# Fetching routing weights from DRAM instead of spreading them with TensorE, for two early row blocks of a soft mixture of experts

## The chip, the core and the metric

The kernel runs on one core of a Trainium2 chip. The metric is the device time of one execution in microseconds, from the first to the last instruction. A core has TensorE (PE in the profile, with its weight loads as PEld), VectorE (DVE), ScalarE (ACT), GpSimd (POOL) and SyncE (SP). SP issues most of the DMAs, on a hardware queue (q1 in the profile); GpSimd issues those that change the type of the data, on a software queue (q0). Both queues are served by the same 16 DMA engines.

## What is computed

Each token has a softmax over eight experts, and its output is the sum of all eight experts' products, weighted by that softmax.

```python
probs = softmax(router_logits)              # 16 x 512 tokens, 8 experts
output = zeros(16, 512, 2048)
for e in range(8):
    output += probs[:, :, e:e+1] * (x @ expert_weights[e])   # 512 -> 2048
```

The kernel uses that a routing weight may be multiplied into x first. With z_e = p_e x, the whole is one matrix product of 8192 rows (tokens), an inner length of 8 x 512 = 4096, and 2048 columns.

## The kernel before

**The work as a whole.** The big product is cut in two by two by two (256-row blocks with an even and an odd number, experts 0 to 3 and 4 to 7, the left and the right 1024 columns), and a seven-product scheme (Strassen-Winograd) takes the place of the eight block products. Several of those products are cut in the same way again inside: `sub_product` (L370) takes two row blocks, forms four products z of x and routing weights with `mul` (L344), four sums and differences of them, and from these runs seven inner products p1 to p7 of two times eight matmuls (once for each 128 rows). The inner operands are named in the table `z` there: p1 takes a11, p2 a12, p5 s1, p6 s2, p3 s4, p7 the difference a11 - a21, p4 a22; they run in this order. Matmuls are fp16, 128 x 128 by 128 x 512, and add up in fp32 in the eight PSUM banks. Intermediate results go to DRAM (`kept`).

**The order of the work.** Almost all DVE and ACT instructions of the start are pinned to the order in which the program writes them (`dve`, L114). Within an engine instructions run in order. DMAs are placed on their queue by a scheduler, and a DMA that must wait holds up everything behind it on the queue of the engine that issues it. Buffers of the pool `h` are handed out by hand: `share` (L78) gives each use those that were taken longest ago.

**How the kernel starts.** Eight tiles of 128 rows of x lie in `xs0`: four of row blocks 0 and 2, four of row blocks 4 and 6. In row terms the second four are 1024 to 1279 and 1536 to 1791.

- The first four tiles get their routing weights by TensorE: x is multiplied with a diagonal matrix of the weights (`diag`, L250; `early_z0`, L269), which transposes and weights it in one step. Their product runs plainly in the loop over `n` from L442, in two halves of 512 columns.
- The second four tiles must become what `sub_product` wants: x transposed (`xT`), and the routing weights of each token spread over all 128 partitions (`pT`). `early_xp1` (L284) does both with TensorE during the second half of that loop: four matmuls with the identity give a transposed tile, and one matmul of a matrix of ones with four diagonals side by side gives the spread weights. DVE evicts the first from PSUM, ACT the second. The weights for it come from a small softmax of these rows alone (`early_p(1)`), from logits that have been loaded for it in the right layout.
- All later blocks take another way. `softmax_of_all` (L308) computes the routing weights of all rows and writes them with four stores to `p_dram` (L297), in a layout from which `load_p` (L339) fetches a block's weights with one DMA that repeats them on every partition.

After the loop, `sub_product(1, 0, P1, ...)` (L480) runs over the row blocks 4 and 6 first, with `xp1` handed to it, and then over later ones, which it loads itself. Between its first operations on DVE lie three sums of weights (`inner_sums`, L173) that p5, p6 and p7 need.

Of the kernel before, what the change touches and what calls it, by code (L numbers as in the profile page):

```python
# [32 lines left out]
def kernel(  # L33
# [7 lines left out]
    nc = tc.nc  # L41
    P = 128
    f16 = mybir.dt.float16
    f32 = mybir.dt.float32
# [4 lines left out]
    E, _, EH = expert_weights.shape  # L49
    T = B * S  # L50
    C = H // P
    HE = E // 2
# [3 lines left out]
    HQ = 256  # L56
# [10 lines left out]
    xpool = ctx.enter_context(tc.tile_pool(name="xpool", bufs=8))  # L67
    hpool = ctx.enter_context(tc.tile_pool(name="hpool", bufs=1))
    cpool = ctx.enter_context(tc.tile_pool(name="cpool", bufs=1))
# [8 lines left out]
    def share(**sizes):  # L78

        order = sorted(used, key=used.get)  # L80
        for use, n in sizes.items():
            places[use], order = [order[:n], 0], order[n:]

    def h_tile(shape, dtype, use="any"):
        mine, i = places[use]
        places[use][1] = (i + 1) % len(mine)
        used[mine[i]] = next(turn)
        return hpool.tile(shape, dtype, name="h", tag=f"h{mine[i]}")
# [22 lines left out]
    def note(i):  # L111
        last[i.ins.engine] = i.ins

    def dve(i):  # L114
        note(i)
        if pinned[0]:
            tc.keep_in_program_order(i)
# [3 lines left out]
    def tt(o, a, b, op):  # L121
        dve(nc.vector.tensor_tensor(out=o, in0=a, in1=b, op=op))  # L122
# [9 lines left out]
    def sp(o, i):  # L132
        note(nc.sync.dma_start(out=o, in_=i))  # L133
# [4 lines left out]
    def bank():  # L138
        return psum.tile([P, NB], f32, name="ps", tag="ps")

    def mm(ps, z, w, start, stop):
        nc.tensor.matmul(ps, z, w, start=start, stop=stop, skip_group_check=True)  # L142
# [5 lines left out]
    def new_w():  # L148
        return wpool.tile([P, K8, NB], f16, name="w", tag="w")
# [23 lines left out]
    def inner_sums(b, t3=None):  # L173

        t3 = t3 or b[0, 1]
        w = {1: b[0, 0], 2: b[1, 0], 3: b[1, 1], 7: t3}

        def step(p, x, y):
            if p not in w:
                w[p] = new_w()  # L180
            tt(w[p], x, y, SUB)
        return w, [lambda: step(5, b[0, 1], b[0, 0]), lambda: step(6, b[1, 1], w[5]),
                   lambda: step(4, w[6], b[1, 0]), lambda: step(7, b[1, 1], b[0, 1])]
# [12 lines left out]
    def softmax(lg, J, pf=None):  # L196
        mx = h_tile([P, J], f32)
        dve(nc.vector.tensor_reduce(out=mx, in_=lg, axis=AX, op=mybir.AluOpType.max))
        tt(lg, lg, mx.unsqueeze(2).to_broadcast([P, J, E]), SUB)
        nc.scalar.activation(out=lg, in_=lg, func=mybir.ActivationFunctionType.Exp)  # L200
        sm = h_tile([P, J], f32)
        dve(nc.vector.tensor_reduce(out=sm, in_=lg, axis=AX, op=ADD))
        dve(nc.vector.reciprocal(out=sm, in_=sm))
        if pf is None:
            pf = h_tile([P, E, J], f32)
        n = pf.shape[1]
        tt(pf, lg.rearrange("p j e -> p e j")[:, 0:n], sm.unsqueeze(1).to_broadcast([P, n, J]), MUL)
        return pf

    lg_f = router_logits.flatten_outer_dims()  # L210
    P2, P1, PQ = 0, HE, 2 * HE
# [6 lines left out]
    def cast_x(j):  # L218
        pool(xs0[:, ds(j, 2), :], x_f[ds(j * HQ, HQ), :].rearrange(ROWS[j // 4], p=P))

    def load_lg0(t):
        rows = lg_f.rearrange("(q h) e -> q h e", h=2 * HQ)[ds(2 * t, 2), 0:HQ]
        tile_ = lg0[t].rearrange("p (q j) e -> p q j e", j=2)
        if t == 0:
            sp(tile_, rows.rearrange("q (p j) e -> p q j e", p=P))
        else:
            for q in range(2):
                sp(tile_[:, q], rows[q].rearrange("(j p) e -> p j e", p=P))
    lg0 = [cpool.tile([P, 4, E], f32, name=f"lg0_{t}") for t in range(2)]
    load_lg0(0)  # L230
    cast_x(0)
    cast_x(2)
    ident = cpool.tile([P, P], f16, name="ident")
# [10 lines left out]
    for e in range(2):  # L244
        cast_w(11, BLOCKS[3], e, b11[BLOCKS[3]])

    def early_p(t):
        return softmax(lg0[t], 4, cpool.tile([P, HE, 4], f16, name=f"ph0_{t}"))

    def diag(p):  # L250

        d = h_tile([P, 4, P], f16)
        tt(d, ident.unsqueeze(1).to_broadcast([P, 4, P]), p.to_broadcast([P, 4, P]), MUL)
        return d

    def evacuate(o, ps, i):
        if i % 2:
            act(nc.scalar.copy(o, ps))
        else:
            dve(nc.vector.tensor_copy(o, ps))  # L260


    z0 = [zpool.tile([P, HE, C, P], f16, name="z", tag="z") for j in range(4)]
    ph0 = [early_p(0)]

    def diag_e(e):
        return diag(ph0[0][:, e].unsqueeze(2))

    def early_z0(e, d):  # L269
        for j in range(4):  # L270
            ps = bank()
            for c in range(C):
                mm(ps[:, ds(c * P, P)], xs0[:, j, ds(c * P, P)], d[:, j], c == 0, c == C - 1)
            evacuate(z0[j][:, e], ps.rearrange("p (c t) -> p c t", c=C), j)


    ones = cpool.tile([P, P], f16, name="ones")
    nc.vector.memset(ones, 1.0)
    xp1 = [[xpool.tile([P, C, HQ], f16, name=name, tag="x") for name in ("xT", "pT")] for t in range(2)]

    def diag_j(j):
        return diag(ph0[1][:, :, ds(j % 4, 1)])

    def early_xp1(j, d):  # L284
        t, rows = j // 2 - 2, ds(j % 2 * P, P)
        ps = bank()
        for c in range(C):
            mm(ps[:, ds(c * P, P)], xs0[:, j, ds(c * P, P)], ident, c == 0, c == C - 1)
        evacuate(xp1[t][0][:, :, rows], ps.rearrange("p (c t) -> p c t", c=C), 0)
        ps = bank()  # L290
        mm(ps, ones, d.rearrange("p e t -> p (e t)"), True, True)
        evacuate(xp1[t][1][:, :, rows], ps.rearrange("p (e t) -> p e t", e=HE), 1)


    R = 4
# [4 lines left out]

    def load_logits():
        dve(nc.vector.memset(lg_all[:, 0, 0:1], 0.0))
        dve(nc.vector.memset(lg0[1][:, 0, 0:1], 0.0))
        load_lg0(1)
        for r in range(R):
            sp(lg_all[ds(r * NHQ, NHQ)], lg_v[r])

    def softmax_of_all():  # L308
        pf = softmax(lg_all, J)
        ph = h_tile([P, 3 * HE, J], f16)  # L310
        nc.scalar.copy(ph[:, 0:HE], pf[:, HE:E])
        nc.scalar.copy(ph[:, HE:2 * HE], pf[:, 0:HE])
        tt(ph[:, 2 * HE:], pf[:, 0:HE], pf[:, HE:E], ADD)
        for r in range(R):
            sp(p_dram[:, :, ds(r * J, J)], ph[ds(r * NHQ, NHQ)])
# [3 lines left out]
    x_new = []  # L319
# [19 lines left out]
    def load_p(h, first):  # L339
        pT = xpool.tile([P, HE, HQ], f16, name="pT", tag="x")  # L340
        sp(pT, p_dram[h, ds(first, HE), :].partition_broadcast(P))
        return pT
# [10 lines left out]
    def half(use="any"):  # L353
        return h_tile([P, NB], f32, use)
# [82 lines left out]
    ds_ = [diag_e(0), diag_e(1)]  # L437
# [4 lines left out]
    for n in range(2):  # L442
        ps = [bank() for _ in range(4)]
        for e in range(HE):
            if n == 0 and e < 2:
                early_z0(e + 2, ds_[e + 2])
                if e == 0:
                    ds_.append(diag_e(3))
            for c in range(C):
                for j in range(4):  # L450
                    mm(ps[j], z0[j][:, e, c], b11[e // 2, n][:, e % 2 * C + c, :],
                       e + c == 0, e == HE - 1 and c == C - 1)
            if n == 1:
                for j in ((4, 5), (6, 7), (), ())[e]:
                    early_xp1(j, ds_[j - 4])
                if e == 1:
                    sums[0]()
        for j in range(4):
            o = half()
            act(nc.scalar.copy(o, ps[j]))  # L460
            sp(kept[1][j // 2][n].rearrange("(p j) m -> j p m", j=2)[j % 2], o)
        if n == 0:
            ph0.append(early_p(1))
            softmax_of_all()
            ds_ = [diag_j(j) for j in range(4, 8)]
            w, sums = inner_sums(b11, new_w())

    def weights_of_t1():
# [6 lines left out]
        yield  # L475
        ready[5] = yield from inner_weights(b)
    pinned[0] = False
    x_new.extend((4 + 2 * t, xp1[t][0]) for t in range(2))
    share(xs=3, r=4, o=8)
    sub_product(1, 0, P1, w, weights_of_t1(), 1,  # L480
                xp1, (sums[1], sums[3], sums[2]))
# [115 lines left out]
    rows = Rows(0)  # L597
# [9 lines left out]
    for q in range(NI):  # L607
# [14 lines left out]
        for j, tn in enumerate(QUARTERS):  # L622
            if j > 1:
                rows.load_kept(j)
            x = bank()
# [34 lines left out]
        for j, tn in enumerate(QUARTERS):  # L660
            x, m5 = xs[j], rows.m5[tn]
# [17 lines left out]
        if q == 0:  # L679
# [15 lines left out]
            rows = following  # L695
            continue

        def prod(p, b):
            if b not in banks:
                banks[b] = bank()  # L700
            for k in range(K8):
                mm(banks[b], z3[p][:, k, :], inner3[p][:, k, :],
                   p in (1, 5) and k == 0, k == K8 - 1)
            return banks[b]
# [6 lines left out]
        x = prod(1, "x")  # L711
# [15 lines left out]
        if q < NI - 1:  # L727
            d = prod(4, "d")
# [3 lines left out]
        rows = following  # L732
# [35 lines left out]
```

## Time and profile before

| what | value |
|---|---|
| time, median of 3 runs | 1434.25 us (1433.23 to 1434.26) |
| profiled span | 1434.2 us |
| PE busy | 1424.9 us, 99% |
| DVE busy | 1032.0 us, 72% |
| ACT busy | 271.0 us, 19% |
| matmuls of z and weights, 128 x 512 and like it | 6560, 379 ns each from start to end |
| granted TensorE clock | 0.999 of full speed |
| DMA moved | 318.92 MB, mean 222 GB/s |

Busy shares are means over the whole span, and successive matmuls overlap in them. So the table tells which engine sets the pace, and not what happens in a stretch of a few microseconds. For that the timeline is read: each of its rows gives the start, the length, the engine, the line, the operation with output and inputs, the number of instructions merged, and in brackets how long the engine was idle before and what ended the wait. `L122` is the helper of all DVE operations on two tensors, `L142` that of all matmuls, `L133` and `L136` those of the DMAs of SP and GpSimd; which operation is meant is seen from the tiles. In the first 50 us the DMA engines are nearly full up to about 36 us with the first weights and x.

### The profile page before, as it was taken

How to read it: one execution, taken by the hardware profiler on the slowest of the kernel's cores; microseconds unless marked ns; L12 is line 12 of the kernel's file. 1: busy time of each engine (PE TensorE's matmuls, PEld its weight loads, DVE VectorE, ACT ScalarE, POOL GpSimd, SP SyncE). 2: the span in 40 equal slices, each digit the busy share in tenths (PEclk: the TensorE clock that was granted, in tenths of full speed). 3: DMA queues.
4: the chain of work that ended last, by engine and by line, in shares of the span. 5: the costliest groups of instructions: out<-in, count | busy, mean ns of one | idle time of the engine just before them, and what ended most of it. 6: DMA issues, size and time to landing. Idle time of an engine off the chain costs nothing.

```text
span 1434.2 us, 18172 instructions
## 1 busy us (share of the span) xinstructions
PE 1424.9 (99%) x6654; PEld 647.9 (45%) x6654; DVE 1032.0 (72%) x1173; ACT 271.0 (19%) x472; POOL 219.6 (15%) x344
## 2 busy tenths in 40 slices
PE   9999999999999999999999999999999999999998
PEld 4444444444444444444444444444444444444444
DVE  6967585656686867766767687777777877877773
ACT  3211111111111111111111211111111111111111
POOL 3111000110001000001000222222222222222220
PEclk9999999999999999999999999999999999999999
DMA  9899967899649994467766967777777767778764
GB/s 196 185 249 266 274 160 191 183 258 259 208 148 301 352 338 147 132 191 222 213 248 206 298 188 238 237 237 233 229 220 226 210 212 214 231 234 242 220 199 103
DMA packets 192041, 318.92 MB, mean 222 GB/s; under 512 B 51664, under 2 KB 80592, under 8 KB 187344
## 3 DMA queue, kind: packets, MB, share of 16 engines
q1 hardware_dynamic: 135328, 202.92, 44.2%
q0 software_dynamic: 56624, 114.84, 34.1%
q8 instruction: 52, 0.85, 0.2%
q14 instruction: 37, 0.30, 0.1%
HBM read 180.13 MB, written 159.58 MB: 237 GB/s over the span
## 4 chain that ended last, share of the span: by engine, by line
PE 93%; issue 3%; DMA 2%; POOL 1%; DVE 0%; ACT 0%; POOLq 0%; SPq 0%; DVEq 0%; ACTq 0%
PE ps L142 93%; POOL out_dram L595 1%; DMA h<-kept 1%; DMA out_dram<-h 1%; DMA w<-in_expert_weights_dram 1%; POOL w L136 0%; DVE z L122 0%; DVE h L122 0%; ACT ps L626 0%; SPq L133 0%; POOLq L595 0%; POOL ident L235 0%; DVEq L122 0%; POOLq L136 0%; POOLq L235 0%
## 5 line engine op out<-in xcount | busy, mean ns | idle before, releaser
L142 PE MATMUL ps<-w,z 128*128 128x512 f16 x6560 | 1415.2, 379 | 3.5 <-ACT ps L626 1.9
L142 PEld LDWEIGHTS <-z 128*128 128x128 f16 x6560 | 641.6, 98 | 776.0 <-issue 2.2
L122 DVE TENSOR_TENSOR h<-ps,h 128x512 f32<-128x512 f32 x389 | 267.7, 689 | 312.9 <-PE ps L142 89.2
L122 DVE TENSOR_TENSOR z<-xT,pT 128x2048 f16<-128x2048 f16 x252 | 304.2, 1218 | 32.5 <-PE ps L142 30.5
L122 DVE TENSOR_TENSOR z<-z 128x2048 f16<-128x2048 f16 x280 | 303.6, 1108 | 7.3
L404 ACT COPY h<-ps 128x512 f32<-128x512 f32 x248 | 145.3, 586 | 602.1 <-PE ps L142 594.9
L595 POOL DMA_DIRECT2D out_dram<-h x244 | 153.7, 663 | 535.4 <-DVE h L122 328.8
L122 DVE TENSOR_TENSOR w<-w 128x4096 f16<-128x4096 f16 x36 | 82.3, 2286 | 0.8 <-DMA w<-wd 0.7
L664 ACT COPY h<-ps 128x512 f32<-128x512 f32 x64 | 37.5, 585 | 177.0 <-PE ps L142 172.4
L136 POOL DMA_DIRECT2D h<-in_x_dram x30 | 21.3, 709 | 263.3 <-DMA xT<-h 226.2
L122 DVE TENSOR_TENSOR h<-h 128x512 f32<-128x512 f32 (+1 forms) x67 | 46.0, 687 | 20.8 <-DMA h<-kept 20.3
L122 DVE TENSOR_TENSOR h<-h,ps 128x512 f32<-128x512 f32 (+1 forms) x78 | 52.7, 675 | 11.0 <-PE ps L142 10.9
L136 POOL DMA_DIRECT2D w<-in_expert_weights_dram x41 | 30.8, 765 | 187.3 <-DVE w L161 131.0
L645 ACT ACTIVATE ps<-h 128x512 f32<-128x512 f32 x35 | 21.0, 602 | 166.9 <-DVE h L122 166.9
L626 ACT COPY ps<-h 128x512 f32<-128x512 f32 x64 | 35.6, 593 | 36.3 <-DMA h<-kept 30.7
L136 POOL DMA_DIRECT2D w<-wd x12 | 6.5, 543 | 189.1 <-DVE w L161 116.1
L724 ACT COPY h<-ps 128x512 f32<-128x512 f32 x15 | 8.8, 585 | 120.7 <-PE ps L142 120.7
L713 ACT COPY h<-ps 128x512 f32<-128x512 f32 x15 | 8.8, 586 | 16.5 <-PE ps L142 16.5
L260 DVE CAST z<-ps 128x512 f16<-128x512 f32 x8 | 5.2, 686 | 4.3 <-PE ps L142 4.3
L136 POOL DMA_DIRECT2D w<-wdt x8 | 4.4, 560 | 21.9 <-DVE w L161 21.9
L260 DVE CAST xT<-ps 128x512 f16<-128x512 f32 x4 | 2.6, 687 | 5.4 <-PE ps L142 5.4
L142 PEld LDWEIGHTS <-w 128*128 128x128 f16 x80 | 5.0, 98 | 2.6 <-DMA w<-in_x_dram 0.9
(37 smaller groups left out, 44.3 us busy)
## 6 DMA issues: line engine op xcount, KB each, us to landing
out_dram<-h POOLq DMA_DIRECT2D x244, 256.0 KB, 4.9
kept<-h SPq DMA_DIRECT2D x192, 256.0 KB, 4.1
h<-kept SPq DMA_DIRECT2D x192, 256.0 KB, 4.6
pT<-p_dram SPq DMA_DIRECT2D x124, 256.0 KB, 5.1
w<-in_expert_weights_dram POOLq DMA_DIRECT2D x39, 512.0 KB, 12.8
out_dram<-h SPq DMA_DIRECT2D x75, 256.0 KB, 3.4
xT<-x SPq DMA_DIRECT2D x62, 256.0 KB, 2.8
w<-wd POOLq DMA_DIRECT2D x12, 1024.0 KB, 10.7
```

The source lines that it names most:

```text
L122: dve(nc.vector.tensor_tensor(out=o, in0=a, in1=b, op=op))
L136: note(nc.gpsimd.dma_start(out=o, in_=i))
L142: nc.tensor.matmul(ps, z, w, start=start, stop=stop, skip_group_check=True)
L260: dve(nc.vector.tensor_copy(o, ps))
L404: nc.scalar.copy(t, ps)
L595: queue.dma_start(out=out_rows(self.q, odd, tn[0], cols, tn[1]), in_=o, **how)
L626: act(nc.scalar.copy(x, rows.m1[tn]))
L645: act(nc.scalar.mul(banks[b], v, scale))
L664: act(nc.scalar.copy(c21, x))
L713: act(nc.scalar.copy(r1, x))
L724: act(nc.scalar.copy(r3, x))
```

## The change

The routing weights of the row blocks 4 and 6 are now fetched from `p_dram` by `load_p`, as for all later blocks. TensorE only transposes their x. The small softmax, its logits' loads, the matrix of ones and the four diagonals of these rows are gone. The eviction of the four transposed tiles, once all on DVE, alternates between DVE and ACT. It is meant to relieve PE of four matmuls, DVE of the diagonals and the softmax, and ACT of two evictions.

```diff
-    def load_lg0(t):
-        rows = lg_f.rearrange("(q h) e -> q h e", h=2 * HQ)[ds(2 * t, 2), 0:HQ]
...
-    lg0 = [cpool.tile([P, 4, E], f32, name=f"lg0_{t}") for t in range(2)]
-    load_lg0(0)
+    lg0 = cpool.tile([P, 4, E], f32, name="lg0")
+    sp(lg0.rearrange("p (q j) e -> p q j e", j=2),
+       lg_f.rearrange("(q h) e -> q h e", h=2 * HQ)[0:2, 0:HQ].rearrange("q (p j) e -> p q j e", p=P))
...
-    ones = cpool.tile([P, P], f16, name="ones")
-    nc.vector.memset(ones, 1.0)
-    xp1 = [[xpool.tile([P, C, HQ], f16, name=name, tag="x") for name in ("xT", "pT")] for t in range(2)]
-
-    def diag_j(j):
-        return diag(ph0[1][:, :, ds(j % 4, 1)])
-
-    def early_xp1(j, d):
+    x1 = [xpool.tile([P, C, HQ], f16, name="xT", tag="x") for t in range(2)]
+
+    def early_x1(j):
         t, rows = j // 2 - 2, ds(j % 2 * P, P)
         ps = bank()
         for c in range(C):
             mm(ps[:, ds(c * P, P)], xs0[:, j, ds(c * P, P)], ident, c == 0, c == C - 1)
-        evacuate(xp1[t][0][:, :, rows], ps.rearrange("p (c t) -> p c t", c=C), 0)
-        ps = bank()
-        mm(ps, ones, d.rearrange("p e t -> p (e t)"), True, True)
-        evacuate(xp1[t][1][:, :, rows], ps.rearrange("p (e t) -> p e t", e=HE), 1)
+        evacuate(x1[t][:, :, rows], ps.rearrange("p (c t) -> p c t", c=C), j)
...
     def load_logits():
         dve(nc.vector.memset(lg_all[:, 0, 0:1], 0.0))
-        dve(nc.vector.memset(lg0[1][:, 0, 0:1], 0.0))
-        load_lg0(1)
...
                 for j in ((4, 5), (6, 7), (), ())[e]:
-                    early_xp1(j, ds_[j - 4])
+                    early_x1(j)
...
         if n == 0:
-            ph0.append(early_p(1))
             softmax_of_all()
-            ds_ = [diag_j(j) for j in range(4, 8)]
+            xp1 = [(x1[t], load_p(4 + 2 * t, P1)) for t in range(2)]
             w, sums = inner_sums(b11, new_w())
...
-    x_new.extend((4 + 2 * t, xp1[t][0]) for t in range(2))
+    x_new.extend((4 + 2 * t, x1[t]) for t in range(2))
```

More of the change, by code (lines that the diff above doesn't have):

```diff
@@ L219, in cast_x @@
         pool(xs0[:, ds(j, 2), :], x_f[ds(j * HQ, HQ), :].rearrange(ROWS[j // 4], p=P))
-    def load_lg0(t):
-        rows = lg_f.rearrange("(q h) e -> q h e", h=2 * HQ)[ds(2 * t, 2), 0:HQ]
[L223 to L228, printed above, removed]
-    lg0 = [cpool.tile([P, 4, E], f32, name=f"lg0_{t}") for t in range(2)]
-    load_lg0(0)
+    lg0 = cpool.tile([P, 4, E], f32, name="lg0")
+    sp(lg0.rearrange("p (q j) e -> p q j e", j=2),
+       lg_f.rearrange("(q h) e -> q h e", h=2 * HQ)[0:2, 0:HQ].rearrange("q (p j) e -> p q j e", p=P))
     cast_x(0)
@@ L245 @@
         cast_w(11, BLOCKS[3], e, b11[BLOCKS[3]])
-    def early_p(t):
-        return softmax(lg0[t], 4, cpool.tile([P, HE, 4], f16, name=f"ph0_{t}"))
     def diag(p):
@@ L263 @@
     z0 = [zpool.tile([P, HE, C, P], f16, name="z", tag="z") for j in range(4)]
-    ph0 = [early_p(0)]
+    ph0 = softmax(lg0, 4, cpool.tile([P, HE, 4], f16, name="ph0"))
     def diag_e(e):
-        return diag(ph0[0][:, e].unsqueeze(2))
+        return diag(ph0[:, e].unsqueeze(2))
     def early_z0(e, d):
```

## The prediction

> **What bounds the kernel now.** I read the page's busy shares first: PE 99% of 1434.2 us, DVE 72%, ACT 19%. So TensorE (PE) sets the end, and a change counts only by the matmuls it takes away and the waits it gives PE. Then the chain of waits over the first 100 us, because the edit touches only that stretch (columns: start, length, what):
>
> ```profile
> 10.80 35.64 PE ps L142 x188
> 46.44 0.78 issue
> 47.21 1.23 DVE z L122
> 48.44 0.05 issue
> 48.49 51.54 PE ps L142 x238
> ```
>
> PE runs without a break from 10.80, but at 48.49 it has waited for VectorE (DVE) to write a z tile. The PE timeline gives the size of that hole:
>
> ```profile
> 34.18 13.98 PE L142 MATMUL ps<-w,z 128*128 128x512 f16 x64
> 48.49 17.87 PE L142 MATMUL ps<-w,z 128*128 128x512 f16 x82 [0.33 <-DVE z L122]
> ```
>
> One matmul shows 0.379 us from start to end (its row on the page), so 64 of them start (13.98 - 0.379) / 63 = 0.2159 us apart; the 65th could have started at 34.18 + 64 x 0.2159 = 48.00. The hole is 0.49 us. The first 32 of these 64 are the end of the first product; from 41.09 follow the seven sub-products of the first two row blocks, eight matmuls (1.73 us) each, in the order p1, p2, p5, p6, p3, p7, p4. Matmul 65 is p3, and its operand is s4. The DVE timeline shows s4 as the last of a chain:
>
> ```profile
> 29.39 1.29 DVE L260 CAST xT<-ps 128x512 f16<-128x512 f32 x2 [4.83 <-PE ps L142]
> 30.79 2.36 DVE L122 TENSOR_TENSOR z<-xT,pT 128x2048 f16<-128x2048 f16 x2
> 33.73 1.29 DVE L260 CAST xT<-ps 128x512 f16<-128x512 f32 x2 [0.58 <-PE ps L142]
> 34.93 2.28 DVE L122 TENSOR_TENSOR w<-w 128x4096 f16<-128x4096 f16 x1
> 37.13 2.35 DVE L122 TENSOR_TENSOR z<-xT,pT 128x2048 f16<-128x2048 f16 x2
> 39.40 2.28 DVE L122 TENSOR_TENSOR w<-w 128x4096 f16<-128x4096 f16 x1
> 41.60 1.22 DVE L122 TENSOR_TENSOR z<-z 128x2048 f16<-128x2048 f16 x1
> 42.74 2.29 DVE L122 TENSOR_TENSOR w<-w 128x4096 f16<-128x4096 f16 x1
> 44.94 3.49 DVE L122 TENSOR_TENSOR z<-z 128x2048 f16<-128x2048 f16 x3
> ```
>
> From 33.73 to 48.43 DVE never rests, so here it is the bound, and everything hangs on when its first product with pT (30.79) may start. In the kernel before, pT came from PE and ScalarE (ACT) and was there in time. Last, the queue of SyncE (SP), with the times from issue to landing below it (median):
>
> ```profile
> 22.47 2.67 SPq L133 DMA_DIRECT2D p_dram<-h  x4
> 25.68 3.06 SPq L133 DMA_DIRECT2D kept<-h  x4
> ...
> p_dram<-h SPq DMA_DIRECT2D x4, 48.0 KB, 8.8
> ...
> kept<-h SPq DMA_DIRECT2D x4, 256.0 KB, 10.9
> ```
>
> These stores are slow because the 16 DMA engines are full with the weights and x of the other queue until about 34 (section 2 of the page: DMA 9 there). One by one, the p_dram stores took 6.7, 7.4, 8.8 and 10.1 us: the last, issued at 24.52, landed at 34.6. The last kept store, issued at 28.2, landed at 39.1. They landed in the order of issue.
>
> **What the Trainium skill says.** "DMA: Bandwidth & Descriptors", section "Queues, rings and completion order": each DMA engine serves the queue rows in turn, packet by packet, and takes the descriptors of one ring in order. The trace agrees: while the software queue was busy, p_dram's 1536 small packets crept through at some 190 per us, and the kept stores landed only behind them. The same page, "Two DMAs through the same engine are not ordered": a load of what an earlier DMA wrote must wait for that DMA's semaphore before it is issued. So load_p has to sit on SP until p_dram has landed. "TensorE: Matmul & The Clock Gate", section "Back-to-back issue gap", gives 2.5 ns above N / 2.4 for a warm matmul, 215.8 ns for 512 columns; measured 215.9. Its section "What's actually happening" says that an idle window of about 3.4 us halves the clock until about 3.4 us of work; the trace shows a cold start (10 warm-up matmuls in 4.43 us), but no idle time that long afterwards.
>
> **The change, part by part.**
>
> Taken from PE: four matmuls of ones with a diagonal, 4 x 0.2159 = 0.86 us. Taken from DVE: four diagonals (2.49 us at 22.07) and the small softmax (five operations from 15.89 to 17.20), plus memsets. The diagonals are worth nothing themselves, as DVE then waits until 29.39 for PE. The small softmax stood ahead of the large one; without it the large one can start when the last eviction ends at 15.98 instead of at 17.20. The logits (landed by 16.0, and without the many small pieces of the other load no later) don't hold it. So p_dram is written 1.2 us earlier: issued from 21.25, last landing 34.6 - 1.2 = 33.4.
>
> Moved: of the eight evictions four stay, two on DVE and two on ACT. DVE had four in the chain above; one of the two at 33.73 goes, 0.6 us of the chain after the first product.
>
> Added: two loads of pT, 256 KB each. In the changed kernel's instruction order they stand on SP's queue behind the four kept stores and wait for all four p_dram stores. SP is through with kept at 28.74, then stands until 33.4. Behind the loads stand the transposes of the next blocks' x, first needed much later (their product ran at 51.75). The loads go at 33.4 and about 33.9 into the ring behind 1 MB of kept, whose last store landed at 39.1. Two corrections of that: p_dram is 1.2 us earlier, so kept is too. And x's third load, which GpSimd (POOL) issued at 39.63 after waiting 17.97 us for a kept store to free its buffer, now has a buffer that waits for no store. So it goes out near 23, as soon as an earlier load on its lane has landed, and its 256 KB, about 1.3 us at the 205 GB/s that this stretch moved, take turns with kept. The two cancel: kept lands near 39.2. pT then needs one more transfer's time. The four kept stores landed from 36.7 to 39.1, 0.8 us apart, so pT lands at about 40.0 and the second at 40.8. **T = 40.0** is when DVE may start. Bounds: 33.4 plus the 3.1 us of the fastest pT load in the trace, 36.5; and 42 if the three queues' work adds up without overlap.
>
> DVE's sequence from there, with the steps as they were: both products take until T + 2.27 before the next operation starts, one eviction 0.6, then the stretch from 34.93 to 48.43 unchanged, 13.5. So s4 is ready at T + 16.4 and p3 starts then. It started at 48.49, so the loss is T + 16.4 - 48.49 = T - 32.1; at T = 40.0 that is **7.9 us**. The second pT is needed only at T + 5.1, when it is there. PE meets the wait in pieces: p1 waits for a11 until 41.2 (without the ones matmuls it could start at 40.2), p5 for s1 until T + 10.8 = 50.8 (p2 ends about 44.7: a hole of 6.1), p6 for s2 until 54.1 and p3 for s4 until 56.4. The 0.86 us that PE saves lie inside these holes and bring nothing. p4 needs its weights at T + 18.6 and starts at T + 19.9, so nothing more is lost. A hole of 6.1 us may halve the clock: p5 would then take 3.4 instead of 1.7 us, which fits ahead of s2; if it stayed cold through p6, some 1.2 us would be lost in addition. I take 0 for it and keep 1.2 for the range.
>
> Does the loss stay? After this PE runs without a hole to 842.9, and its chain there goes back to PE's own results; a delay at 48 shifts everything. DVE is late by as much, but the next blocks' operands had slack: the last one was ready at 63.0 for a p3 due at about 72.6. Sum: 1434.25 + 7.9 = 1442.2.
>
> **Rivals.** (B) pT passes the kept stores or they are quicker: T = 36.5, loss 4.4, 1438.7. For it: round-robin service and 400 GB/s once the weights are in. Against: one ring, landed in order. (C) pT is there when DVE wants it, T about 30.3: then the hole of 0.49 closes and 0.86 us of matmuls are gone, 1434.25 - 1.4 = 1432.9. For it: p_dram is issued at 21.25, nine microseconds ahead. Against: its own landing at 34.6. (D) The loss arises but a later wait takes it up, such as the 1.88 us at 842.9, which would have to shrink fully and more: about 1436.0. Against: that wait hangs on PE's own pace. (E) T = 42 and a cold clock: 9.9 + 1.2 = 11.1, 1445.4.
>
> **How the numbers follow.** Forecast 0.66, B 0.17, C 0.04, D 0.05, E 0.08. The range 1438.2 to 1444.6 takes in B and most between the forecast and E; it leaves out C, D and the end of E, with some spread around B. Only C and D lie within 0.2% (2.9 us): same 0.08; nothing found brings more than 1.4 us: faster 0.02; slower 0.90.
>
> **What would show it.** In the changed profile: the first product z<-xT,pT near 40 instead of 30.79, with DVE idle before it and pT from p_dram as releaser; PE idle some 9.3 us (7.9 + 0.49 + 0.86) in three or four pieces between 40 and 57; last p_dram landing near 33.4; SP's pT issues just after it; a third x load near 23. I am wrong if the first product starts near 30, if SP issues pT before 30, or if the later profile makes up for the delay.

## The result, and the profile after

| | median | runs | ratio to before |
|---|---|---|---|
| before | 1433.59 us | 6, 1433.05 to 1434.26 | |
| changed | 1445.22 us | 6, 1443.84 to 1446.53 | 1.0079, 95% interval 1.0066 to 1.0092 |

The change costs 11.6 us (9.5 to 13.2 by the interval). The forecast was 7.9, with a range up to 1444.6: the direction and the path (VectorE waiting for pT) were right, and the size was too small. The profiled spans are 1434.2 and 1443.3 us, only 9.1 apart. Where the other 2.5 us are is part of what follows.

The timeline of DVE in the changed kernel (start, length, engine, line, operation, count, idle time before and what ended it):

```profile
28.67 0.69 DVE L250 CAST xT<-ps 128x512 f16<-128x512 f32 x1 [7.71 <-PE ps L142]
41.20 2.36 DVE L122 TENSOR_TENSOR z<-xT,pT 128x2048 f16<-128x2048 f16 x2 [11.84 <-ACT h L440]
43.48 0.68 DVE L250 CAST xT<-ps 128x512 f16<-128x512 f32 x1
44.08 2.28 DVE L122 TENSOR_TENSOR w<-w 128x4096 f16<-128x4096 f16 x1
...
54.09 3.49 DVE L122 TENSOR_TENSOR z<-z 128x2048 f16<-128x2048 f16 x3
```

The eviction is over at 29.36, and DVE then stands for 11.84 us until its first product with pT: T = 41.20. The releaser that is named, an ACT copy, is a trap. Copies at line 440 write stage buffers, which the product doesn't read; the wait is for several semaphores at once and is put down to the event that came last. SP's queue shows what it was:

```profile
21.27 2.67 SPq L133 DMA_DIRECT2D p_dram<-h  x4
24.95 2.70 SPq L133 DMA_DIRECT2D kept<-h  x4
34.22 0.81 SPq L133 DMA_DIRECT2D pT<-p_dram  x2
```

And the DMA view has the time from issue to landing of the two loads (last column, the median):

```profile
pT<-p_dram SPq DMA_DIRECT2D x2, 256.0 KB, 7.0
```

The first load was issued at 34.22, when the last p_dram store had landed, and took 6.9 us: 41.1. In e_kept_act and the other variants with a load below, the same wait is put down to pT's load itself. PE:

```profile
42.49 5.01 PE L142 MATMUL ps<-w,z 128*128 128x512 f16 x16 [2.83 <-DVE z L122]
52.03 5.32 PE L142 MATMUL ps<-w,z 128*128 128x512 f16 x16 [4.53 <-DVE z L122]
57.64 2.55 PE L142 MATMUL ps<-w,z 128*128 128x512 f16 x11 [0.29 <-DVE z L122]
```

p1 and p2 wait for the first products (2.83 us), p5 for s1 (4.53 us), p3 for s4. p3 starts at 57.64, which is T + 16.44; the forecast had T + 16.4.

### The profile page after: what moved, and what is told of

It reads as the page before. It is cut to its first block, busy times and chain, and to the rows that moved or that the text cites. A ratio compares the mean times of both kernels' runs of the same rounds, so it can differ in the third digit from the quotient of the medians.

```text
span 1443.3 us, 18144 instructions
## 1 busy us (share of the span) xinstructions
PE 1426.7 (99%) x6650; PEld 647.9 (45%) x6650; DVE 1027.0 (71%) x1160; ACT 270.0 (19%) x469; POOL 219.7 (15%) x344
## 3 DMA queue, kind: packets, MB, share of 16 engines
q0 software_dynamic: 56624, 114.84, 33.9%
## 4 chain that ended last, share of the span: by engine, by line
PE 90%; issue 4%; DMA 1%; DVE 1%; POOL 1%; ACT 0%; SPq 0%; POOLq 0%; DVEq 0%; ACTq 0%
PE ps L142 90%; POOL out_dram L574 1%; DMA out_dram<-h 1%; DMA h<-kept 1%; DVE z L122 0%; DVE h L122 0%; DVE w L122 0%; POOL w L136 0%; DVE xT L250 0%; ACT ps L605 0%; SPq L133 0%; POOLq L574 0%; DVEq L122 0%; POOLq L136 0%; ACTq L605 0%
## 5 line engine op out<-in xcount | busy, mean ns | idle before, releaser
L605 ACT COPY ps<-h 128x512 f32<-128x512 f32 x64 | 35.5, 593 | 38.2 <-DMA h<-kept 34.8
```

Source lines behind the costliest of these rows:

```text
L605: act(nc.scalar.copy(x, rows.m1[tn]))
```

## The experiments

One sum holds in the profiles, and the table uses it: **span = start of p3 + PE's late wait + 1383.8 us**, with the late wait being the single hole of PE near 842 us in the kernel before (852 in the changed one). The last number is the same to within 0.1 us in twelve of the fourteen profiles: after p3, the rest of the program takes the same time.

| run | first product on PE | T | start of p3 | late wait | span |
|---|---|---|---|---|---|
| before, first profile | 10.80 | - | 48.49 | 1.88 | 1434.2 |
| before_again | 9.80 | - | 47.47 | 0.37 | 1431.7 |
| before_again2 | 10.29 | - | 47.97 | 0.69 | 1432.5 |
| before_again3 | 10.07 | - | 47.75 | 1.51 | 1433.1 |
| changed, first profile | 10.08 | 41.20 | 57.64 | 1.88 | 1443.3 |
| after_again | 10.49 | 41.78 | 58.22 | 1.19 | 1443.2 |
| e_kept_act | 10.23 | 42.01 | 58.44 | 1.70 | 1444.0 |
| e_x_late | 9.74 | 38.95 | 55.8 by the sum | 0.91 | 1440.5 |
| e_pt_before_kept | 10.10 | 38.22 | 54.65 | 1.64 | 1440.1 |
| e_both | 10.09 | 38.56 | 54.99 | 1.29 | 1440.1 |
| e_small_first | 9.53 | 33.20 | 49.63 | 1.24 | 1435.0 |
| e_small_first2 | 10.06 | 34.26 | 50.70 | 1.34 | 1436.1 |
| e_const | 10.11 | 29.92 | 47.09 | 1.52 | 1432.5 |
| e_hole | 9.34 | - | 46.53 by PE's pace | none | 1430.3 |

Where T is the bound and the table has p3 from the trace, p3 - T is 16.43 or 16.44 in all seven. In the two forms of e_small_first the rest takes 0.3 us longer than the sum has it. That lies behind the last matmul: from its end to the end of the span they take 4.1 us, the first profiles of the kernel before and of the changed one 3.9.

### The kernel before, three times more

No edit.

> The kernel before once more, unchanged, for a second profile of it. The profiled span of the first was 1434.2 us, but its execution took 1435.99 us, while the six timed ones took 1433.05 to 1434.26. If the first profile was of a slowish execution, this one shows a span near 1432.3 and p3 of the first blocks starts well before 48.49 (near 46.8). If the profile was typical, p3 starts within 0.3 us of 48.49 again and the span is near 1434.

> The kernel before, unchanged, a third profile, for the spread of two things: the start of the first product on PE (10.80 and 9.80 us so far) and PE's wait near 842 (1.88 and 0.37 us). p3 should lie 37.7 us after that start, and the span be p3 + that wait + 1383.8, whatever the two are. If the change lengthened the late wait (its kernels showed 0.91 to 1.88), it should stay below 0.9 here; if it is chance, anything from 0.4 to 1.9.

> The kernel before, unchanged, a fourth profile, with the same question as the third: p3 37.7 us after the first product, and the late wait below 0.9 us if the change is what lengthens it, anything from 0.4 to 1.9 if it is chance.

They took 1433.45, 1434.27 and 1434.87 us. p3 is 37.7 us after the first product each time (37.67 to 37.69), as PE and DVE work through that stretch without a DMA in their way. The first product itself comes between 9.80 and 10.80, as the first x and weights land. The timeline of PE in before_again, to be compared with that of the prediction:

```profile
9.80 3.62 PE L142 MATMUL ps<-w,z 128*128 128x512 f16 x16
...
47.47 14.85 PE L142 MATMUL ps<-w,z 128*128 128x512 f16 x68 [0.33 <-DVE z L122]
```

So the profile on which the prediction rests was one with a late start. The late wait is 0.37, 0.69, 1.51 and 1.88 us in four executions of one kernel. The changed kernel and its variants lie in the same band, 0.91 to 1.88. Their mean is 0.3 us higher; whether the change adds to it can't be told from so few.

### The changed kernel once more

No edit.

> The changed kernel once more, unchanged, for a second profile: how far T (the start of DVE's first product with pT, 41.2 in the first profile) and PE's wait near 852 (1.88 us) vary from execution to execution. If T is set by full DMA engines as read, it lies within 1 us of 41.2, and p3 16.4 us after it. If the wait near 852 is a matter of chance, as the two profiles of the kernel before suggest (1.88 and 0.37 us), it differs by half a microsecond or more; if the change brought it, it stays at 1.7 to 2.

T = 41.78, 0.6 us from the first profile, and p3 16.44 us later; time 1444.94. The late wait is 1.19 instead of 1.88, which speaks for chance.

### No wait: pT without a load

```diff
...
-            xp1 = [(x1[t], load_p(4 + 2 * t, P1)) for t in range(2)]
+            xp1 = [(x1[t], p1c[t]) for t in range(2)]     # p1c: filled with 0.125 by GpSimd
```

> The changed kernel with pT of the row blocks 4 and 6 filled with 0.125 by GpSimd instead of loaded: it leaves out the routing weights of these two blocks in the first inner product, and with them the wait. Theory W (the whole loss is the wait of DVE's first product for pT): with the wait gone the product starts near 29.5, the hole ahead of p3 closes, and the four matmuls are gained: 1.0 to 1.9 us below before. Rival R (the rest of the change costs something too: other order of DMAs on SP, an earlier third load of x, other buffers): it stays 1 us or more above before.

1433.61 us against 1433.75, ratio 0.9996 (0.9988 to 1.0005). The loss is gone, so rival R falls: with the two loads and the wait for them away, the rest of the change costs nothing that can be measured (0.7 us at the most by the interval). The gain of 1.0 to 1.9 us was not found by timing either. In the trace p3 is 36.98 us after the first product instead of 37.68, so 0.70 us were gained, and a wait of PE for weights near 14.7, which is there in some executions and not in others, took 0.33 more. In the chain of waits s4, the last z, still ends just ahead of p3:

```profile
45.81 1.23 DVE z L122
47.04 0.05 issue
47.09 13.12 PE ps L142 x60
```

The hole doesn't close, because DVE's chain begins with PE's second pair of transposes. Of the matmuls taken away, the two ahead of that pair move the chain (0.43 us), and the spared eviction shortens it (0.60): together 1.03, which is 0.70 + 0.33.

### Kept stores in another ring

```diff
-            sp(kept[1][j // 2][n].rearrange("(p j) m -> j p m", j=2)[j % 2], o)
+            q = nc.scalar if n == 0 else nc.sync
+            note(q.dma_start(out=kept[1][j // 2][n].rearrange("(p j) m -> j p m", j=2)[j % 2], in_=o))
```

> The changed kernel with the four kept stores of the first column half issued by ACT, so that they lie in another ring than the loads of pT, which keep their wait for p_dram. Theory F (pT's data stand behind 1 MB of kept in one ring): the loads go at 34.2 as before, but are then served beside kept, and pT lands near 39.0 instead of 41.1; the first product starts 1.5 to 2.5 us sooner and the time is that much below the changed kernel, some 1443. Rival G (p_dram's landing and the filled DMA engines alone set it): pT lands at 40.5 or later, the time moves by under 0.7 us.

Theory F fails. Rival G has pT's landing right (40.5 or later), but not what moved. SP's queue:

```profile
21.28 2.67 SPq L133 DMA_DIRECT2D p_dram<-h  x4
37.35 0.84 SPq L133 DMA_DIRECT2D pT<-p_dram  x2
```

The DMA view of the moment in which the last p_dram store was issued, and then of the four kept stores:

```profile
p_dram<-h SPq DMA_DIRECT2D x1, 48.0 KB, 14.0
...
kept<-h ACTq DMA_DIRECT2D x4, 256.0 KB, 5.8
```

With kept out of the way, the pT loads were quicker (4.7 us instead of 7.0). But kept, now in a third ring (the queue of its own that ACT issues to, beside those of SP and GpSimd), was served beside p_dram's small pieces instead of behind them: the last store took 14.0 us instead of 10.9 and landed at 37.3. T = 42.0. Time 1444.30 us, 10.6 above before (ratio 1.0067, 1.0053 to 1.0080). Here a ring of its own gave the stores no more of the DMA engines in sum: what kept gained, p_dram paid.

### pT ahead of kept

```diff
+        if n == 0:
+            softmax_of_all()              # p_dram stores, pT loads and kept stores
+            xp1 = [(x1[t], load_p(4 + 2 * t, P1)) for t in range(2)]   # now in this order on SP
         for j in range(4):
             o = half()
             act(nc.scalar.copy(o, ps[j]))
...
         if n == 0:
-            softmax_of_all()
-            xp1 = [(x1[t], load_p(4 + 2 * t, P1)) for t in range(2)]
...          # and these stores and loads are pinned to this order
```

> The changed kernel with SP's order fixed by hand: the four p_dram stores, then the two loads of pT, then the four kept stores. So pT has no kept in front of it and none beside it, but still waits for all of p_dram. It parts the delay of pT into p_dram's landing and what comes after. Theory F (kept ahead in the ring costs pT some 3 us): p_dram lands at 33.5 to 34.5, pT some 4 us later, T = 37.5 to 38.5, and the time is 2.5 to 3.5 us below the changed kernel. Rival G (after p_dram has landed a pT load takes 6 to 7 us whatever lies ahead of it): T above 40 and under 1 us gained.

SP's queue:

```profile
33.74 0.84 SPq L136 DMA_DIRECT2D pT<-p_dram  x2
34.67 2.25 SPq L136 DMA_DIRECT2D kept<-h  x4
```

The landing of its loads, from the DMA view:

```profile
pT<-p_dram SPq DMA_DIRECT2D x2, 256.0 KB, 4.5
```

And DVE's first product, from its timeline:

```profile
38.22 2.36 DVE L122 TENSOR_TENSOR z<-xT,pT 128x2048 f16<-128x2048 f16 x2 [8.52 <-DMA pT<-p_dram]
```

Theory F holds. The loads are issued when they were before, half a microsecond apart at most, and take 4.5 us instead of 7.0. T falls by 3.3 us from the mean of the two profiles of the changed kernel (41.49). The time is 1441.86 us, 7.7 above before (ratio 1.0047, 1.0032 to 1.0062). Of the delay of T, some 3 us are kept in front of pT; the larger part is the wait for p_dram's landing at 33.7 and the load after it.

### x's third load held back

```diff
     share(xs=3, r=4, o=8)
+    places["xs"][0][2], places["r"][0][1] = places["r"][0][1], places["xs"][0][2]
```

> The changed kernel with one pair of buffers swapped, so that x's third load has to wait for a kept store to land, as it did in the kernel before; it goes out near 40 instead of 23. Theory X (its 256 KB take turns with kept and hold pT up by 1.3 us): T near 40.0, and the time 1 to 1.5 us below the changed kernel. Rival: these bytes find room between the others, T within 0.4 us of 41.2 and the time unchanged.

GpSimd's issue of the load in the changed kernel and in this one, and DVE's first product here:

```profile
22.93 0.72 POOL L136 DMA_DIRECT2D h<-in_x_dram  x1 [1.82 <-DMA w<-in_expert_weights_dram]
...
37.32 0.71 POOL L136 DMA_DIRECT2D h<-in_x_dram  x1 [16.56 <-DMA kept<-h]
...
38.95 2.36 DVE L122 TENSOR_TENSOR z<-xT,pT 128x2048 f16<-128x2048 f16 x2 [9.93 <-DMA pT<-p_dram]
```

The last kept store in the DMA view, first of the changed kernel (issued at 27.06), then of this one (issued at 26.62):

```profile
kept<-h SPq DMA_DIRECT2D x1, 256.0 KB, 12.8
...
kept<-h SPq DMA_DIRECT2D x1, 256.0 KB, 11.6
```

The load goes out at 37.32 instead of 22.93, and T = 38.95: 2.5 us less than the mean of the changed kernel, twice what theory X had. The last kept store lands at 38.2 instead of 39.8, and pT 0.6 us behind it instead of 1.2 and 1.9. (0.4 of the 2.5 us were there already when p_dram had landed, at 33.7 instead of 34.0 in the mean.) Time 1442.53 us, 8.4 above before (1.0053, 1.0039 to 1.0066). Here alone the clock shows in the result: by the sum p3 is at 55.8, while s4 was ready at T + 16.4 = 55.4. After a hole of 5.92 us p5 and most of p6 ran at half the clock (granted 0.50 from 48.5 to 55) and came late to p3.

### Both at once

The two edits above together (the buffer being the one of a kept store in this order).

> Both remedies at once: pT's loads ahead of kept on SP, and x's third load held back until a kept store has landed. Each alone brought T from 41.5 (mean of two profiles) to 38.2 and 38.9. If they take away separate costs, T goes to the floor that the rival B of the prediction named: p_dram landed (33.7) and a pT load in nearly free DMA engines (3.1 us or little more), 36.8 to 37.4; time 1 us below the run with pT ahead of kept alone. If both took away the same cost (DMA engines shared with other work while pT moves), T stays at 38.2 within 0.5.

The landing of the loads in the DMA view, and the first product in DVE's timeline:

```profile
pT<-p_dram SPq DMA_DIRECT2D x2, 256.0 KB, 4.6
```

```profile
38.56 2.36 DVE L122 TENSOR_TENSOR z<-xT,pT 128x2048 f16<-128x2048 f16 x2 [9.19 <-DMA pT<-p_dram]
```

T = 38.56, no better than with the first edit alone; 1441.61 us, 7.3 above before (1.0050, 1.0036 to 1.0063). The two take away the same cost, kept's data in front of pT: one by moving pT ahead, the other by letting kept through sooner. What stays is a load of 4.5 us, not the 3.1 of the quickest in the trace. Rival B's floor was too low by that.

### Small stores first

```diff
+        for r in range(R):
+            i = nc.sync.dma_start(out=p_first[:, :, ds(r * J, J)], in_=ph[ds(r * NHQ + 4, 3), P1:P1 + HE])
...
+            i = nc.sync.dma_start(out=pT, in_=p_first[2 * t].partition_broadcast(P))
...          # and only then the four p_dram stores, and kept
```

> The changed kernel with the routing weights of row blocks 4 to 6 stored first, in four stores of 12 pieces of 128 bytes to a tile of their own, then the two loads of pT from that tile, and only then the four large p_dram stores and kept. Theory P (pT is late because it waits for 1536 small pieces of p_dram, then for kept): the small stores land near 26.5, the loads go near 27 and land at 31 to 32; the first product starts there, p3 near 48, and the time is 0 to 1.5 us below before. Rival Q (any way through DRAM is too slow while the DMA engines are full): the small stores take 8 us as well, pT lands at 36 or later, and the time is 4 us or more above before.

> The run with the small stores first once more; in the first form of it these stores took the weights of experts 4 to 7 where those of 0 to 3 belong, and here they take the right ones. Sizes and order are the same. There pT landed at 33.2 and the time was 3.2 us above before; the same is expected here, T 32.5 to 34 and 2.5 to 3.8 us above before. If the first form was off for another reason, it differs by over 1 us.

The edit shown is that of the second form; the first form has `0:HE` in its place, and so stores the weights of experts 4 to 7 where those of 0 to 3 belong.

1436.92 us in the first form (ratio 1.0021, 1.0014 to 1.0028) and 1437.55 in the second (1.0021, 1.0015 to 1.0028): 3.2 and 3.4 us above before. SP's queue in the second, and then DVE's first product:

```profile
21.38 3.15 SPq L296 DMA_DIRECT2D p_first<-h  x4
28.66 0.83 SPq L302 DMA_DIRECT2D pT<-p_first  x2
```

```profile
34.26 2.36 DVE L122 TENSOR_TENSOR z<-xT,pT 128x2048 f16<-128x2048 f16 x2 [4.62 <-DMA pT<-p_first]
```

Neither theory is right in full. 48 pieces instead of 1536 let the loads go 5.6 us sooner than in the changed kernel, so the small pieces are about half of the delay (T would be near 30 without a wait). But even for four stores of 1.5 KB SP waits until 7.3 us after the first was issued, and the loads take 6 us beside the software queue, which still fills the DMA engines with weights and x (205 GB/s then). The way through DRAM needs some 13 us here, and from the end of the softmax to the moment when DVE wants pT there are about 9.

### The hole in the kernel before

```diff
-        evacuate(xp1[t][0][:, :, rows], ps.rearrange("p (c t) -> p c t", c=C), 0)
+        evacuate(xp1[t][0][:, :, rows], ps.rearrange("p (c t) -> p c t", c=C), int(j == 7))
```

> The kernel before with one edit: of the four evictions of the second pair of tiles, the last of x goes to ACT instead of DVE. It tests whether DVE's chain of operations sets p3 in the kernel before, as read: then the hole of 0.49 us ahead of p3 closes, p3 starts 37.2 instead of 37.7 us after the first product, and the time falls by that 0.5 us, which timing can hardly show. If PE's hole came from elsewhere, p3 stays at 37.7 after the first product.

The timeline of PE:

```profile
32.71 37.50 PE L142 MATMUL ps<-w,z 128*128 128x512 f16 x173
```

PE runs through where the 65th of these matmuls had waited. p3 would be at 32.71 + 64 x 0.2159 = 46.53, 37.19 us after the first product: the hole is closed, and DVE's chain was its cause. This execution had no late wait at all. Time 1433.22 us against 1434.34, ratio 0.9993 (0.9985 to 1.0002): it may be faster than both kernels, but the timing doesn't show it.

## Why the prediction was right or wrong

- **What bounds the stretch, and the rule loss = T + 16.4 - start of p3**: right. 16.43 or 16.44 in seven profiles with T from 33.2 to 42.0 (in e_x_late alone the clock adds 0.4), and e_hole closes the hole as the reading of DVE's chain requires. So the failure lies in T and in p3 of the kernel before, not in the rule.
- **PE's savings lie inside the holes**: right in the changed kernel. In e_const, where nothing covers them, the edit is worth 1.0 us at p3 (of which the wait for weights took 0.33) and not the 1.4 of rival C: C added the closing of the hole to all four matmuls, but DVE's chain still ends last, and it hangs on the second transposes.
- **p_dram 1.2 us earlier, the loads behind kept, x's third load moved to 23**: all three are in the trace (21.27 against 22.47; issue order; 22.93). That the load on SP waits for the full p_dram, as the Trainium skill's "DMA: Bandwidth & Descriptors" has it under "Two DMAs through the same engine are not ordered", is what SP's gap up to 34.22 shows (the last p_dram store landed at 34.2). The same page's "Queues, rings and completion order" (rows served in turn) fits e_kept_act: a third ring took its share from p_dram.
- **T = 40.0**: mis-sized; this is the step that failed. T was 41.20 and 41.78, 1.5 us more in the mean. In both profiles the last kept store landed at 39.8 and not at 39.2, the first pT load 1.2 and 1.9 us behind it and not 0.8, and the product began 0.1 us after that. What was wrong is "the two cancel": p_dram's lead of 1.2 us was to bring kept forward by as much, and x's third load to hold it back by 1.3. The lead was there: the last p_dram store landed at 34.2 and 33.9 in the changed kernel and at 33.7 in e_x_late, where it was 35.2 to 35.5 in the four profiles of the kernel before. But the last kept store, which had landed at 39.1, 38.2, 37.9 and 37.9 there (38.3 in the mean), landed later and not at the same time. e_x_late, where x's third load is out of the way as in the kernel before, parts the two: kept landed at 38.2. So x's third load cost kept up to 1.6 us and pT another 1.0, and against the mean of the four p_dram's lead brought kept nothing. Against the first profile alone, from which the forecast was made, the lead brought 0.8 us. This parting rests on one profile of e_x_late. Why the lead doesn't reach kept was not tested; it would fit that the same bytes of weights, x, p_dram and kept have to pass the same DMA engines, whichever goes first.
- **p_dram's landing**: misread. It was put at 34.6 in the kernel before, from "6.7, 7.4, 8.8 and 10.1"; but the last three of these were means over two neighbouring stores. Alone, the four took 6.7, 8.1, 9.4 and 10.8, the last landing is 35.4, and 34.2 follows for the changed kernel, where 34.2 was measured. In the forecast this moved only SP's issue of pT, as T was counted from kept; for rival B's floor it is 0.8 us.
- **The cold clock**: it came (granted clock 0.54 in the stage from 52 to 54 us), and cost nothing in the changed kernel, as taken: p5 was done before s2. It cost 0.4 us only in e_x_late. It also came sooner than forecast: after the first hole, of 2.83 us, the clock was 0.58 of full speed from 42 to 46, and p1 and p2 took 5.01 us; in after_again, after a hole of 2.78 us, they took 3.63 at the full clock. So a pause shorter than the 3.4 us that the prediction cites can be enough here, and isn't always.
- **The start of p3 in the kernel before, 48.49**: mis-sized too. The first profile started 0.57 us later than the mean of the four (p3 47.92), and T was counted from DMA landings and not from PE's start, so this took as much from the forecast loss. A sign of it was to be had: that execution took 1435.99 us, more than any of the three timed ones. But the same profile also had the last kept store 0.8 us later than the mean of the four (39.1 against 38.3), which raised the forecast of T. With both means the same working gives 39.2 + 16.4 - 47.9 = 7.7: two accidents of one profile nearly cancelled, and more profiles of the kernel before would not have mended the forecast.
- **The late wait stays as it is**: unsettled. Two profiles of the changed kernel have 1.54 in the mean, four of the one before 1.11; the spread within one kernel is larger than this.

So the sum becomes 57.93 - 47.92 = 10.0 us at p3 (7.9 + 1.5 + 0.6), and 10.4 with the late wait, which lies within the measured 9.5 to 13.2. The other 1.2 of the 11.6 us lie in which executions were profiled: the four of the kernel before took 1434.65 us in the mean, against the median of 1433.59 of the six in the result (1433.75, 1434.13 and 1434.34 in the later comparisons), and the two of the changed kernel 1445.0 against 1445.22. Whether that is more than chance is not shown. Rival E, 11.1, came closest in number, in part by luck: its T of 42 was nearly right, but its clock cost of 1.2 wasn't there. B and C failed on their landing times, D on the fixed 1383.8 us after p3.

## What to carry to other kernels

A value that goes to DRAM and comes back costs the store's landing and the load's landing, one after the other, at the prices of that stretch: here 13 us and 7 us with full DMA engines, in exchange for matmuls worth 0.9 us. When a change swaps engine work for a transfer, first write down when the value is needed, and count back from there. When a transfer shares full DMA engines with others, don't count on one store's lead to pass on to the next: in e_x_late p_dram landed over 1 us earlier than in the kernel before, and the last kept store no earlier than in the mean there. And when the loss is a difference of two times, take both from more than one profile: here p3 was 0.6 us and kept's landing 0.8 us late in the one that was used.

## What the runs showed of the hardware that I had not expected

- Four stores of 1.5 KB, 12 pieces each, let the loads that wait for them go only 7.3 us after the first was issued, while the software queue kept the DMA engines full; four of 48 KB in pieces of 128 bytes, 13 us (21.27 to 34.2).
- Giving the kept stores their own ring made the p_dram stores slower, 14.0 instead of 10.9 us for the last one.
- Moving one load of 256 KB out of the full stretch made another transfer land 2.5 us earlier (0.4 of it before p_dram had landed), although at 205 GB/s its bytes take 1.3 us by the prediction's estimate.
- TensorE's clock halved after a pause of 2.83 us in one execution of the changed kernel and not after one of 2.78 us in another.
